# Attention weights copied by DMA to float32r tiles and transposed as float32r, in pairs 1 to 6

## The chip, the core and the metric

The kernel runs on one core of one Trainium2 chip. The metric is the device time of one execution in microseconds (us). Before the change it is 680.45 us, the median of three runs (680.29 to 680.69).

## The reference

One layer over a sequence of 1024 positions and a width of 1024. A normalised and modulated input goes through one combined projection into two groups of eight heads of width 64. Both groups compute causal attention in blocks of 128 queries; each block makes a matrix of weights, 128 queries by up to 1024 keys, and multiplies it with the values (forgetting attention first, then stick-breaking):

```python
s = jnp.einsum('bhqd,bhkd->bhqk', q, k).astype(jnp.float32) * scale
s = s + (f_q[..., :, None] - f_k[..., None, :])
causal = k_pos[None, :] <= q_pos[:, None]
s = jnp.where(causal, s, -jnp.inf)
p = jax.nn.softmax(s, axis=-1)
return jnp.einsum('bhqk,bhkd->bhqd', p.astype(v.dtype), v)
...
later = lax.cumsum(log_keep, axis=3, reverse=True) - log_keep
w = jnp.where(strict, jnp.exp(log_beta + later), 0.0)
return jnp.einsum('bhqk,bhkd->bhqd', w.astype(v.dtype), v)
```

The gated head outputs go through one output projection, are added to the residual with a gate, and are normalised.

## The kernel before

The sixteen heads are worked on as eight pairs. Pairs 0 to 3 are stick-breaking, pairs 4 to 7 forgetting attention. A unit is (pair, head in the pair, block of 128 queries); there are 128 units, 16 in a pair. Block i of a unit sees (i + 1) x 128 keys, so a unit's weights are a tile of 128 rows and 128 to 1024 columns.

TensorE's order is written out by hand: one loop over turns k (at the end of `tile_hybrid_layer`). In a turn of pairs 0 to 3 `weights_turn(k)` comes first, then `scores_turn(k)`, then a piece of the projections of later pairs ("fill"; tiles `m` at L312 to L314 and `v` at L370 to L372). In a turn of pairs 4 to 7 the scores come first, then a fill, then the weights, then another fill. `scores_turn(k)` issues the score products of unit k into PSUM tile S (L483, L484). `weights_turn(k)` transposes the weights of unit k - 2 (LAG = 2; L537, into PSUM tile T, four blocks of 128 x 128 to a tile) and multiplies with the values what is complete (L554).

Between scores and transposes a unit runs through the other engines:

- pairs 0 to 3: ScalarE makes two sigmoids (L506 to tile kp, L508 to tile be), VectorE scans kp (L514, L518), GpSimd multiplies be by kp (L520) and zeroes one column (L521, which may stand ahead of L520). Then be is what is transposed.
- pairs 4 to 7: VectorE adds the forget row fb and finds the row's extreme (L491, to tile a), ScalarE exponentiates (L496), VectorE takes a reciprocal (L497), GpSimd scales (L499). Then a is what is transposed.

A transpose is a TensorE product in transpose mode: the block of weights is loaded as the stationary operand (LDWEIGHTS, the rows PEld), a 128 x 128 identity in float32 is streamed through it. ScalarE then rounds T to float32r (L539, tile pt), and VectorE takes what is left over (L540).

The tiles kp, be, a, and the forget rows fb share one tag with six buffers ("att", 128 x 1024 float32 each). The order of the instructions on the other engines, and of the DMAs on the queue of SyncE (SP), is made by a scheduler when the kernel is built. That queue is first in, first out: a DMA that waits for its data holds up those behind it. It carries weight loads (`raw`, L123), copies of keys within SBUF (L298), finished outputs (`y_dr`, L578) and, in pairs 4 to 6, the output weights (`raw_o`, and `wo_dr` at L896, L897).

Of the kernel before, what the change touches and what calls it, by code (L numbers as in the profile page):

```python
# [7 lines left out]

F32 = mybir.dt.float32
F32R = mybir.dt.float32r  # L10
AF = mybir.ActivationFunctionType
ALU = mybir.AluOpType

P = 128
# [3 lines left out]
NPAIR = 8  # L18
# [5 lines left out]
BIG = 3.0e38  # L24
# [3 lines left out]
def tile_hybrid_layer(  # L28
# [17 lines left out]
    nc = tc.nc  # L46

    cp = ctx.enter_context(tc.tile_pool(name="const", bufs=1))
# [4 lines left out]
    def big(tag, bufs, name, dt=F32, shape=None):  # L53
        return sb.tile(shape or [P, 1024], dt, tag=tag, bufs=bufs, name=name)

    def att_tile(name, dt=F32):
        return big("att", 6, name, dt)

    def pt_tile(name, dt=F32R, shape=None):
        return big("pt", 3, name, dt, shape or [P, 2, 1024])  # L60
# [7 lines left out]
    def t_tile(name):  # L68
        return ps.tile([P, 512], F32, tag="T", bufs=2, name=name)

    def s_tile(name):
        return ps.tile([P, 2, 512], F32, tag="S", bufs=1, name=name)
# [11 lines left out]
    def after(*instructions):  # L84
        stack = ExitStack()
        for i in instructions:
            stack.enter_context(tc.issue_after(i.ins))
        return stack


    ident = cp.tile([P, P], F32, tag="ident", name="ident")
    make_identity(nc, ident)
    causal = cp.tile([P, P], F32, tag="causal", name="causal")
    nc.gpsimd.memset(causal, 0.0)
    nc.gpsimd.affine_select(out=causal, in_=causal, pattern=[[-1, P]], base=0,
                            channel_multiplier=1, compare_op=ALU.is_ge, fill=MASKED)
# [9 lines left out]
    gate = cp.tile([P, D], F32, tag="gate", name="gate")  # L106
# [339 lines left out]
    st_w, st_pt = {}, {}  # L446
# [4 lines left out]
    def att_query(u):  # L451
# [3 lines left out]
        r = slice(h * HD, h * HD + HD)  # L455
        nc.scalar.copy(z[r, :], qst[p][h].bitcast(F32)[r, i * P:i * P + P])  # L456

    masks, scaled, lows, gates = [], [], [], []

    def att_causal(u):  # L460
        p, h, i = u
        if p >= 4:
            if not masks:
                masks.append(pv_tile("causal_ps", 1)[:, :P])
                nc.vector.tensor_copy(masks[0], causal)
            f = fb[2 * (p - 4) + h]
            dg = slice(i * P, i * P + P)
            nc.vector.tensor_tensor(f[:, dg], f[:, dg], masks[0], op=ALU.add)

    def att_scores(u, following):  # L470
        p, h, i = u
        z = zq.pop(u)
        ke = (i + 1) * P
        ns = 1 if ke <= 512 else 2
        w = ke // ns
        qs = slice(i * P, i * P + P)
        if p >= 4:
            f = fb[2 * (p - 4) + h]
        S = s_tile(f"S_{p}_{h}_{i}")
        halves = range(ns) if p >= 4 else range(ns)[::-1]  # L480
        for s in halves:
            ks = slice(s * w, s * w + w)
            nc.tensor.matmul(S[:, s, :w], qst[p][h][:, qs], kst[p][h][:, ks], start=True, stop=False)  # L483
            nc.tensor.matmul(S[:, s, :w], z, klo[p][:, ks], start=False, stop=True)  # L484
        v3 = lambda a: a[:, :ke].rearrange("p (a b) -> p a b", a=ns)
        if p >= 4:
            a = att_tile(f"a_{p}_{h}_{i}")
            nm = sb.tile([P, 1], F32, tag="nm", bufs=4, name=f"nm_{p}_{h}_{i}")
            l = sb.tile([P, 1], F32, tag="l", bufs=4, name=f"l_{p}_{h}_{i}")
            with after(*lows):  # L490
                nc.vector.tensor_tensor_reduce(out=v3(a), in0=S[:, :ns, :w], in1=v3(f),  # L491
                                               op0=ALU.add, op1=ALU.min, scale=-1.0, scalar=BIG,
                                               accum_out=nm)
            if following:
                att_causal(following)
            nc.scalar.activation(a[:, :ke], a[:, :ke], AF.Exp, scale=-1.0, bias=nm, accum_out=l)  # L496
            nc.vector.reciprocal(l, l)  # L497
            scaled[:] = [*scaled[-3:],
                         nc.gpsimd.tensor_scalar(a[:, :ke], a[:, :ke], l, 1.0, op0=ALU.mult, op1=ALU.mult)]  # L499
            st_w[u] = a  # L500
        else:
            kp = att_tile(f"kp_{p}_{h}_{i}")
            be = att_tile(f"be_{p}_{h}_{i}")
            with after(*key_casts):
                for s in halves:
                    nc.scalar.activation(kp[:, s * w:s * w + w], S[:, s, :w], AF.Sigmoid, scale=-1.0)  # L506
            key_casts.clear()
            last_act = nc.scalar.activation(v3(be), S[:, :ns, :w], AF.Sigmoid)  # L508
            gates[:] = [last_act]


            lo = ke - w
            rv = kp[:, lo:ke][:, ::-1]
            last_dve = nc.vector.tensor_tensor_scan(rv, rv, floor[:, :ke - lo], initial=0.0,  # L514
                                                    op0=ALU.mult, op1=ALU.max)
            if lo:
                rv = kp[:, :lo][:, ::-1]
                last_dve = nc.vector.tensor_tensor_scan(rv, rv, floor[:, P:P + 1].to_broadcast([P, lo]),  # L518
                                                        initial=kp[:, lo:lo + 1], op0=ALU.mult, op1=ALU.max)
            nc.gpsimd.tensor_tensor(be[:, :ke - 1], be[:, :ke - 1], kp[:, 1:ke], op=ALU.mult)  # L520
            nc.gpsimd.memset(be[:, ke - 1:ke], 0.0)  # L521
            st_w[u] = be
            return last_act, last_dve

    def att_transpose(u, between=()):
        p, h, i = u
        a = st_w.pop(u)
        j, qo = i // 2, (i % 2) * P
        for g in range((i // 4) + 1):
            n = min(4, i + 1 - 4 * g)  # L530
            if (p, h, j, g) not in st_pt:
                st_pt[p, h, j, g] = pt_tile(f"pt_{p}_{h}_{j}_{g}", F32R, [P, 2, 4, 256])
            hi, lo = (st_pt[p, h, j, g][:, x] for x in range(2))
            tp = t_tile(f"T_{p}_{h}_{i}_{g}")
            for b in range(n):
                kb = 4 * g + b
                nc.tensor.transpose(tp[:, b * P:(b + 1) * P], a[:, kb * P:(kb + 1) * P], ident)  # L537
            t3 = tp[:, :n * P].rearrange("p (a b) -> p a b", a=n)
            nc.scalar.copy(hi[:, :n, qo:qo + P], t3)  # L539
            lows[:] = [nc.vector.tensor_tensor(lo[:, :n, qo:qo + P], t3, hi.bitcast(F32)[:, :n, qo:qo + P],  # L540
                                               op=ALU.subtract)]
            while between:
                att_pv(*between.pop(0))
# [3 lines left out]
    def att_pv(p, h, j):  # L547
        acc = pv_tile(f"pv_{p}_{h}_{j}")
        last = 2 * j + 1
        acc2 = acc.rearrange("p (a b) -> p a b", a=2)  # L550
        for kb in range(last + 1):
            pt = st_pt[p, h, j, kb // 4][:, :, kb % 4]
            q0 = P if kb == last else 0
            nc.tensor.matmul(acc2[:, :, q0:], vt[p][:, kb, h * P:(h + 1) * P], pt[:, :, q0:],  # L554
                             start=(kb == 0), stop=(kb == last))
        if p < 4:
            summed.append((acc, p, h, j))
        else:
            att_sum(acc, p, h, j)
# [276 lines left out]
    for kb in range(NB):  # L836
# [9 lines left out]
        if kb < len(evacs):  # L846
            n, h = evacs[kb]
# [237 lines left out]
    def weights_turn(k):  # L1085
        if LAG <= k < len(units) + LAG:
            u = units[k - LAG]
            att_transpose(u, ready)
            seen.add(u)
            if (u[0], u[1], u[2] ^ 1) in seen:  # L1090
                ready.append((u[0], u[1], u[2] // 2))
        while k >= len(units) + LAG and ready:
            att_pv(*ready.pop(0))
# [106 lines left out]
```

## Time and profile before

| what | value |
|---|---|
| median of three runs | 680.45 us |
| span of the profiled execution | 678.6 us |
| TensorE matmul busy | 668.3 us (98%) |
| TensorE weight loads busy | 571.2 us (84%) |
| VectorE, ScalarE, GpSimd busy | 485.9, 382.6, 405.2 us |
| transposes of attention weights | 576 |
| DMAs issued by SP | 294 |

The profiled execution's own time is not listed apart from its span: the span runs from its first to its last instruction, and the median of the three runs is 1.85 us above it, which is taken for what lies around it. Matmuls are pipelined and their ends are modelled, so the starts of successive matmuls tell what one costs, not their busy time. The merged rows of a timeline give the start, the time from the first start to the last end, and how many instructions a row holds.

### The profile page before, as it was taken

The numbers are of one execution on the slowest core, as the hardware profiler recorded it, in microseconds if no ns is written. First come the engines' busy times: TensorE is split into PE (matmuls) and PEld (weight loads), VectorE is DVE, ScalarE is ACT, GpSimd is POOL, SyncE is SP. The second block draws the span as 40 slices with busy tenths as digits, with TensorE's granted clock in tenths as the row PEclk, the third lists the DMA queues.
The fourth block names the chain that finished last, engine by engine and source line by source line (L and its number), as shares of the span: only waits on it lengthen the run. The fifth ranks groups of instructions, "written<-read, shape, count | busy, mean of one in ns | idle before, by whom it ended". The sixth has DMA issues, their size and how long they took to land.

```text
span 678.6 us, 11231 instructions
## 1 busy us (share of the span) xinstructions
PE 668.3 (98%) x3713; PEld 571.2 (84%) x3713; DVE 485.9 (72%) x1001; ACT 382.6 (56%) x889; POOL 405.2 (60%) x530
## 2 busy tenths in 40 slices
PE   8999999999999999999999999999999999999995
PEld 4888898888998888889988888889988888888885
DVE  6787779868677777686776675766676777775645
ACT  5576468757567667576675564655565766521000
POOL 5560279755357556556378878785785365655412
PEclk9999999999999999999999999999999999999998
DMA  9983432112101112122124555263452297153301
GB/s 326 401 312 126 139 79 75 41 28 67 29 20 56 54 42 57 40 54 56 49 93 144 151 164 174 87 201 112 127 169 59 70 350 302 59 177 107 120 32 63
DMA packets 46474, 81.55 MB, mean 120 GB/s; under 512 B 5264, under 2 KB 20176, under 8 KB 46416
## 3 DMA queue, kind: packets, MB, share of 16 engines
q1 hardware_dynamic: 44832, 76.37, 35.1%
q10 hardware_dynamic: 1584, 4.47, 2.1%
q8 instruction: 29, 0.48, 0.3%
q14 instruction: 29, 0.24, 0.1%
HBM read 60.34 MB, written 16.29 MB: 113 GB/s over the span
## 4 chain that ended last, share of the span: by engine, by line
PE 97%; DMA 1%; DVE 0%; POOL 0%; ACT 0%; issue 0%; SPq 0%; POOLq 0%
PE m L312 11%; PE m L314 10%; PE m L313 10%; PE pv L554 10%; PE T L537 9%; PE S L484 5%; PE S L483 5%; PE o L939 4%; PE o L937 4%; PE o L938 4%; PE v L370 4%; PE v L372 4%; PE v L371 4%; PE st_q L647 1%; PE st_k L647 1%; PE st_late L647 1%
## 5 line engine op out<-in xcount | busy, mean ns | idle before, releaser
L540 DVE TENSOR_TENSOR pt<-T,pt 128x512 fp32r<-128x512 f32 (+2 forms) x192 | 102.7, 553 | 43.8 <-ACT pt L539 42.2
L539 ACT CAST pt<-T 128x512 fp32r<-128x512 f32 (+2 forms) x192 | 88.9, 479 | 64.5 <-PE T L537 62.5
L312 PE MATMUL m<-uh,whi 128*128 128x512 f32 x304 | 123.3, 405 | 0.1
L314 PE MATMUL m<-uh,wlo 128*128 128x512 f32 x304 | 119.8, 394 | 0.0
L313 PE MATMUL m<-ul,whi 128*128 128x512 f32 x304 | 119.7, 394 | 0.0
L520 POOL TENSOR_TENSOR be<-be,kp 128x127 f32<-128x127 f32 (+3 forms) x64 | 78.9, 1234 | 36.2 <-DVE kp L518 24.4
L554 PE MATMUL pv<-pt,v 128*128 128x512 f32 x320 | 82.8, 388 | 0.0
L514 DVE TENSOR_TENSOR_SCAN kp<-kp,floor 128x128 f32<-128x128 f32 (+3 forms) x64 | 58.6, 915 | 17.6 <-ACT kp L506 17.4
L499 POOL TENSOR_SCALAR a<-a,l 128x1024 f32<-128x1024 f32 (+3 forms) x64 | 48.4, 756 | 34.3 <-DVE l L497 26.0
L483 PE MATMUL S<-k,q 128*128 128x512 f32 (+5 forms) x192 | 68.8, 360 | 0.0
L314 PEld LDWEIGHTS m<-uh,wlo 128*128 128x128 f32 x304 | 57.1, 188 | 13.7
L496 ACT ACTIVATE a<-a,nm 128x1024 f32<-128x1024 f32 (+3 forms) x64 | 49.8, 779 | 28.6 <-DVE nm L491 28.1
L312 PEld LDWEIGHTS m<-uh,whi 128*128 128x128 f32 x304 | 57.2, 188 | 10.2 <-PE T L537 0.3
L484 PE MATMUL S<-kl,qz 128*128 128x512 f32 (+5 forms) x192 | 65.2, 341 | 0.0
L313 PEld LDWEIGHTS m<-ul,whi 128*128 128x128 f32 x304 | 57.3, 188 | 9.0
L554 PEld LDWEIGHTS pv<-pt,v 128*128 128x128 f32 x320 | 55.5, 189 | 8.9
L570 POOL TENSOR_TENSOR ty<-ty,sg 64x256 f32<-64x256 f32 x64 | 46.9, 733 | 23.4 <-issue 12.2
L491 DVE CUSTOM_DVE_ANT_0 a<-S,fb 128x1024 f32<-128x1024 f32 (+3 forms) x64 | 48.2, 753 | 16.9 <-PE S L484 12.0
L456 ACT CAST qz<-q 64x128 fp32r<-64x128 f32 x128 | 37.3, 296 | 34.2 <-PE S L484 33.0
L506 ACT ACTIVATE kp<-S 128x384 f32<-128x384 f32 (+4 forms) x96 | 44.0, 494 | 21.5 <-PE S L484 20.2
L370 PE MATMUL v<-whi_v,uh 128*128 128x256 f32 (+1 forms) x192 | 54.7, 285 | 0.0
L372 PE MATMUL v<-wlo_v,uh 128*128 128x256 f32 (+1 forms) x192 | 54.2, 282 | 0.0
(296 smaller groups left out, 1628.3 us busy)
## 6 DMA issues: line engine op xcount, KB each, us to landing
raw<-in_w_qkg_dram SPq DMA_DIRECT2D x38, 256.0 KB, 2.7
wss<-in_w_ss_dram SPq DMA_DIRECT2D x14, 512.0 KB, 8.1
x<-in_x_dram SPq DMA_DIRECT2D x8, 512.0 KB, 7.1
k<-k SPq DMA_DIRECT2D x32, 128.0 KB, 2.3
wg<-in_w_gate_dram SPq DMA_DIRECT2D x8, 512.0 KB, 4.9
raw_o<-in_w_out_dram SPq DMA_DIRECT2D x16, 256.0 KB, 3.0
fb<-f_dr ACTq DMA_DIRECT2D x8, 512.0 KB, 4.5
wo_dr<-whi_o SPq DMA_DIRECT2D x16, 256.0 KB, 2.1
```

Source lines behind the costliest of these rows:

```text
L312: nc.tensor.matmul(acc, hi[:, c], u_hi[kt][:, s], start=(kt == 0), stop=False)
L313: nc.tensor.matmul(acc, hi[:, c], u_lo[kt][:, s], start=False, stop=False)
L314: nc.tensor.matmul(acc, lo[:, c], u_hi[kt][:, s], start=False, stop=(kt == NB - 1))
L370: nc.tensor.matmul(acc[:, :n], u_hi[kt][:, ts_], hi[:, s], start=(kt == 0), stop=False)
L372: nc.tensor.matmul(acc[:, :n], u_hi[kt][:, ts_], lo[:, s], start=False, stop=(kt == NB - 1))
L483: nc.tensor.matmul(S[:, s, :w], qst[p][h][:, qs], kst[p][h][:, ks], start=True, stop=False)
L484: nc.tensor.matmul(S[:, s, :w], z, klo[p][:, ks], start=False, stop=True)
L520: nc.gpsimd.tensor_tensor(be[:, :ke - 1], be[:, :ke - 1], kp[:, 1:ke], op=ALU.mult)
L537: nc.tensor.transpose(tp[:, b * P:(b + 1) * P], a[:, kb * P:(kb + 1) * P], ident)
L539: nc.scalar.copy(hi[:, :n, qo:qo + P], t3)
L540: lows[:] = [nc.vector.tensor_tensor(lo[:, :n, qo:qo + P], t3, hi.bitcast(F32)[:, :n, qo:qo + P], op=ALU.subtract)]
L554: nc.tensor.matmul(acc2[:, :, q0:], vt[p][:, kb, h * P:(h + 1) * P], pt[:, :, q0:], start=(kb == 0), stop=(kb == last))
```

## The change

- In pairs 1 to 6 (`HOPS`), each unit's finished weights are copied by a DMA of the SP queue from be or a to another tile of the same tag, declared float32r (`hop`). The copy moves the bytes of (i + 1) x 128 columns as they are.
- The transposes of these pairs read the copy and the identity as float32r and write T as float32r. Pairs 0 and 7 stay as they were.
- The identity is made by the same two GpSimd operations as in the helper used before, written through a float32r tile.
- One unit, (2, 0, 1), is transposed a second time in float32, and the difference of the two, times 3e38, is added to the gate: one more PSUM tile, two transposes, one ScalarE and two VectorE operations.

```diff
+    ident_r = cp.tile([P, P], F32R, tag="ident", name="ident")
+    ident = ident_r.bitcast(F32)
...
+    HOPS = range(1, NPAIR - 1)
+
+    def hop(u, w, ke):
+        if u[0] not in HOPS:
+            return w
+        to = att_tile(f"w_{u[0]}_{u[1]}_{u[2]}", F32R)
+        nc.sync.dma_start(to.bitcast(F32)[:, :ke], w[:, :ke])
+        return to
...
-            st_w[u] = a
+            st_w[u] = hop(u, a, ke)
...
-            st_w[u] = be
+            st_w[u] = hop(u, be, ke)
...
-                nc.tensor.transpose(tp[:, b * P:(b + 1) * P], a[:, kb * P:(kb + 1) * P], ident)
+                if p in HOPS:
+                    nc.tensor.transpose(tp.bitcast(F32R)[:, b * P:(b + 1) * P], a[:, kb * P:(kb + 1) * P], ident_r)
+                else:
+                    nc.tensor.transpose(tp[:, b * P:(b + 1) * P], a[:, kb * P:(kb + 1) * P], ident)
+            if u == (2, 0, 1):
+                tq = t_tile("T_again")
...
+                nc.scalar.copy(ta[:, w], tq[:, w])
+                nc.vector.tensor_tensor(ta[:, w], tp[:, w], ta[:, w], op=ALU.subtract)
+                nc.vector.scalar_tensor_tensor(gate[:, w], ta[:, w], BIG, gate[:, w], op0=ALU.mult, op1=ALU.add)
```

The six buffers now hold in pairs 1 to 3 two of kp, two of be and two copies w, and in pairs 4 to 6 two forget rows, two of a and two copies; each kind takes turns. So a of unit k takes the buffer of a of unit k - 2, which is free once that one's copy has landed.

The queue of SP around the end of pair 1, before: weight loads for pair 3 (`raw_3_...`, the load, its module and half), and outputs of pair 1 (`y_dr`).

```order
L123 DMA raw_3_1_0_2815<-in_w_qkg_dram 128x512
L578 DMA y_dr_91<-ty_1_1_1_2376 64x256
L123 DMA raw_3_1_1_2821<-in_w_qkg_dram 128x512
L123 DMA raw_3_2_0_3003<-in_w_qkg_dram 128x512
L578 DMA y_dr_91<-ty_1_1_2_2490 64x256
L123 DMA raw_3_2_1_3009<-in_w_qkg_dram 128x512
```

The same place in the changed kernel; `w_1_1_6` is the copy of unit (1, 1, 6).

```order
L125 DMA raw_3_1_0_2870<-in_w_qkg_dram 128x512
L466 DMA w_1_1_6_2404<-be_1_1_6_2396 128x896
L602 DMA y_dr_91<-ty_1_1_1_2406 64x256
L125 DMA raw_3_1_1_2876<-in_w_qkg_dram 128x512
L125 DMA raw_3_2_0_3066<-in_w_qkg_dram 128x512
L466 DMA w_1_1_7_2470<-be_1_1_7_2462 128x1024
L466 DMA w_2_0_0_2522<-be_2_0_0_2516 128x128
L602 DMA y_dr_91<-ty_1_1_2_2524 64x256
```

The copies stand between the loads; that of unit (1, 1, 7) stands behind two weight loads.

VectorE at the start of pair 6, before: the reduction of unit (6, 0, 5) (`a_6_0_5`), and the work on the transposes of units (5, 1, 0) and (6, 0, 7) (`pt_... <- T_...`).

```order
L540 TENSOR_TENSOR pt_5_1_0_0_5877<-T_5_1_0_0_5920,pt_5_1_0_0_5877 128x128
L491 ISA a_6_0_5_5946,nm_6_0_5_5947<-S_6_0_5_5941,fb_4_5291 128x768
L491 ISA nm_6_0_5_5947 128x1
L305 SCALAR_TENSOR_TENSOR sg_6_5869<-sg_6_5869,m_6_2_1_5870 128x512
L468 TENSOR_TENSOR fb_4_5291<-fb_4_5291,causal_ps_4030 128x128
L497 RECIPROCAL l_6_0_5_5948<-l_6_0_5_5948 128x1
L540 TENSOR_TENSOR pt_6_0_3_0_5959<-T_6_0_7_0_5960,pt_6_0_3_0_5959 128x4x128
```

The same place in the changed kernel:

```order
L564 TENSOR_TENSOR pt_5_1_0_0_6046<-T_5_1_0_0_6091,pt_5_1_0_0_6046 128x128
L479 TENSOR_TENSOR fb_4_5442<-fb_4_5442,causal_ps_4133 128x128
L508 RECIPROCAL l_6_0_6_6076<-l_6_0_6_6076 128x1
L307 SCALAR_TENSOR_TENSOR sg_6_6038<-sg_6_6038,m_6_2_1_6039 128x512
L564 TENSOR_TENSOR pt_6_0_3_0_6132<-T_6_0_7_0_6133,pt_6_0_3_0_6132 128x4x128
L502 ISA a_6_0_5_6117,nm_6_0_5_6118<-S_6_0_5_6112,fb_4_5442 128x768
L502 ISA nm_6_0_5_6118 128x1
```

The reduction of unit (6, 0, 5) moved behind the first half of the transposed unit (6, 0, 7), whose copy frees the buffer that it writes. The same holds of units (4, 1, 4), (6, 0, 4) and (6, 1, 4). TensorE's order is as before but for the two more transposes.

More of the change, by code (lines that the diff above doesn't have):

```diff
@@ L5 @@
 from concourse import mybir
-from concourse.masks import make_identity
 from concourse._compat import with_exitstack
@@ L88, in after @@
         return stack
-    ident = cp.tile([P, P], F32, tag="ident", name="ident")
-    make_identity(nc, ident)
+    ident_r = cp.tile([P, P], F32R, tag="ident", name="ident")
+    ident = ident_r.bitcast(F32)
+    nc.gpsimd.memset(ident, 0.0)
+    nc.gpsimd.affine_select(out=ident_r, in_=ident, compare_op=ALU.not_equal, fill=1.0, base=0,
+                            pattern=[[-1, P]], channel_multiplier=1)
     causal = cp.tile([P, P], F32, tag="causal", name="causal")
@@ L536, in att_transpose @@
                 kb = 4 * g + b
-                nc.tensor.transpose(tp[:, b * P:(b + 1) * P], a[:, kb * P:(kb + 1) * P], ident)
+                if p in HOPS:
[4 more added lines that the diff above has]
+                tq = t_tile("T_again")
+                for b in range(n):
+                    kb = 4 * g + b
+                    nc.tensor.transpose(tq[:, b * P:(b + 1) * P], a.bitcast(F32)[:, kb * P:(kb + 1) * P], ident)
+                ta = att_tile("T_both")
+                w = slice(0, n * P)
+                nc.scalar.copy(ta[:, w], tq[:, w])
+                nc.vector.tensor_tensor(ta[:, w], tp[:, w], ta[:, w], op=ALU.subtract)
+                nc.vector.scalar_tensor_tensor(gate[:, w], ta[:, w], BIG, gate[:, w], op0=ALU.mult, op1=ALU.add)
             t3 = tp[:, :n * P].rearrange("p (a b) -> p a b", a=n)
```

## The prediction

> **What bounds the kernel now.** First the profile's page: the share of each engine, the clock, and the chain that ended last.
>
> ```profile
> span 678.6 us, 11231 instructions
> PE 668.3 (98%) x3713; PEld 571.2 (84%) x3713; DVE 485.9 (72%) x1001; ACT 382.6 (56%) x889; POOL 405.2 (60%) x530
> PEclk9999999999999999999999999999999999999998
> PE 97%; DMA 1%; DVE 0%; POOL 0%; ACT 0%; issue 0%; SPq 0%; POOLq 0%
> PE m L312 11%; PE m L314 10%; PE m L313 10%; PE pv L554 10%; PE T L537 9%; PE S L484 5%; PE S L483 5%; PE o L939 4%; PE o L937 4%; PE o L938 4%; PE v L370 4%; PE v L372 4%; PE v L371 4%; PE st_q L647 1%; PE st_k L647 1%; PE st_late L647 1%
> ```
>
> The chain is TensorE for 97%, at full clock, and the attention transposes (T L537) are 9% of it. So whatever TensorE is spared counts in full, as long as nothing makes it wait, and every wait that is added counts in full too. Next the busy time by stage, for pairs 1 to 3 (136 to 342 us) and 4 to 6 (342 to 546 us), the two stretches that the change touches.
>
> ```profile
> 136.00:342.00 206.00, 206.00 (x1230) 181.71 (x1229) 152.08 (x261) 135.85 (x328) 118.05 (x164) 1.00 0.18 47
> 342.00:546.00 204.00, 203.95 (x1141) 175.56 (x1141) 139.74 (x366) 120.69 (x293) 149.46 (x170) 1.00 0.44 131
> ```
>
> The columns are the stretch, its length, then busy time of PE, PEld, DVE, ACT, POOL, the clock, the DMA engines' share and GB/s. TensorE has no gap in either; the other engines have a quarter or more of their time free. The view of waits says how near a gap is:
>
> ```profile
> PEld T L537 <- POOL be L520: 1.3, 4, 0.4
> ```
>
> All waiting of TensorE for finished weights is 1.3 us in the whole run. What matters is therefore how early the weights are finished, since the copy comes in between.
>
> **The transposes.** The chain of waits gives what each product costs from one start to the next, around the end of pair 1; then load and product durations by line (LDWEIGHTS is the load; xcount | busy, mean ns | idle), and the one float32 product of 128 columns that is no transpose (L185).
>
> ```profile
> 208.25 0.33 PE T L537 x3
> 208.58 0.06 PE S L483
> 208.64 0.11 PE S L484
> 208.75 0.28 PE m L312
> ...
> 211.35 0.24 PE m L314
> 211.59 0.87 PE T L537 x8
> ```
>
> ```profile
> L484 PEld LDWEIGHTS S<-kl,qz 128*128 128x128 f32 x192 | 36.3, 189 | 3.3
> L537 PEld LDWEIGHTS T<-ident,be 128*128 128x128 f32 x288 | 34.7, 141 | 7.1 <-POOL be L520 1.3 <-POOL be L521 0.4 <-issue 0.3
> ```
>
> ```profile
> L185 PE MATMUL sc_all<-ident,sc x16: 273/275/275, 6.5 to 8.2; 128*128 128x128 f32 x16
> ```
>
> Eight transposes take 0.87 us: 0.109 each. Pairs 1 to 6 have 6 x 2 x 36 = 432, so 47.1 us. A float32r product of 512 columns takes 0.24, so 128 columns stream in 0.06; the transpose streams the same 128 columns in float32 and takes nearly twice that. The other bound is S with 128 columns in float32r: the two S and the excess of the m behind them (0.28 against 0.23 to 0.24) are 0.06 + 0.11 + 0.05 = 0.22 for two, 0.11 each. There it isn't streaming but loads that follow each other, and a load of S takes 189 ns. A transpose's load takes 141, that is 48 less, so at 0.11 the load leaves room and the float32 stream is what fills the time. I take 0.06 (rounded up from 0.058), nearest to the row of 512 columns: **432 x (0.109 - 0.060) = 21.2 us saved**. The ends are 0.11 (nothing saved) and 0.06; a loss is excluded, since S shows float32r with a load of its own for each 128 columns at 0.11. The Trainium skill (FP8 and Floating Point Precision, TensorE Precision Notes) says that true float32 takes four passes through the array, which by quarters would make a transpose 0.027 and the saving 35.4 us; this trace speaks against it, for L185 shows two products for each of the 8 turns of its loop and T L537 one for each transpose (576). The second transpose of unit (2, 0, 1) adds two float32 transposes, 0.2 us, and small work on ScalarE and VectorE; I count 0.3 us. The identity is made by the same two operations: nothing.
>
> **The copies.** Each of 96 units gets a DMA between GpSimd's last step and the first transpose. No 128-row copy inside SBUF is in the trace; the nearest rows (KB each, median us from issue to landing):
>
> ```profile
> fb<-f_dr ACTq DMA_DIRECT2D x8, 512.0 KB, 4.5
> k<-k SPq DMA_DIRECT2D x32, 128.0 KB, 2.3
> out_dram<-r SPq DMA_DIRECT2D x2, 512.0 KB, 2.8
> y_dr<-ty SPq DMA_DIRECT2D x56, 64.0 KB, 1.9
> ```
>
> The same direction is k<-k, 2.3 for 128 KB. From 64 to 512 KB writes out of SBUF rise by 0.9. With 0.1 for the hand-over and the load ahead of the first product I take **c = 2.2 + 1.2 x columns/1024**: 2.35 us for 64 KB, 3.4 for 512 KB. The low end is 2.0 + 0.8 (out_dram), the high end 2.5 + 2.4 (fb, 4.5 for 512 KB, and 0.4 to start).
>
> Against this stands the slack: from the end of GpSimd's last operation on a unit to the start of its first transpose. Four units, GpSimd's rows and TensorE's rows:
>
> ```profile
> 203.08 1.77 POOL L520 TENSOR_TENSOR be<-be,kp 128x895 f32<-128x895 f32 x1 [0.55 <-DVE kp L518]
> 208.32 2.00 POOL L520 TENSOR_TENSOR be<-be,kp 128x1023 f32<-128x1023 f32 x1
> 367.00 0.69 POOL L499 TENSOR_SCALAR a<-a,l 128x512 f32<-128x512 f32 x1
> 492.47 1.14 POOL L499 TENSOR_SCALAR a<-a,l 128x1024 f32<-128x1024 f32 x1
> ```
>
> ```profile
> 206.36 0.60 PE L537 MATMUL T<-ident,be 128*128 128x128 f32 x4
> 211.42 1.03 PE L537 MATMUL T<-ident,be 128*128 128x128 f32 x8
> 374.23 0.60 PE L537 MATMUL T<-ident,a 128*128 128x128 f32 x4
> 495.09 0.60 PE L537 MATMUL T<-ident,a 128*128 128x128 f32 x4
> ```
>
> Unit (1, 1, 6) is ready at 204.85 and transposed from 206.36: slack 1.5, c 3.25. Unit (1, 1, 7): 210.32 and 211.42, 1.1 against 3.4. Unit (4, 0, 3): 367.69 and 374.23, 6.5 against 2.8; it is covered. Unit (6, 0, 7): 493.61 and 495.09, 1.5 against 3.4. I read the slack of all 96 units in this way. The short ones are blocks 6 and 7 in pairs 1 to 3 (0.4 to 1.9 us, the last head of pair 3 excepted), whose chain over four engines is longest, and the start of pair 6; blocks 0 to 4 mostly have 2.5 to 6, and pairs 4 and 5 mostly 4 to 8.
>
> A stall of TensorE moves all that follows on it, so a stall at the unit between a unit's scores and its transposes lengthens that unit's slack. Hence: stall = c + wait in the queue - slack - the stall at the units between + what faster transposes there (0.049 each) bring it forward. (1, 1, 6): unit (1, 1, 5) before it stalls 0.9, with 6 transposes: 3.25 - 1.5 - 0.9 + 0.3 = 1.1. (1, 1, 7) has a wait in the queue as well; its copy now stands behind two weight loads:
>
> ```profile
> 208.26 3.68 SPq L123 DMA_DIRECT2D raw<-in_w_qkg_dram  x2
> ```
>
> The second ends at 211.94 and an issue takes 0.33, so the copy can't start before 211.6, 1.3 after its data: 3.4 + 1.3 - 1.1 - 1.1 + 0.3 = 2.8. (6, 0, 7): 3.4 - 1.5 + 0.1 = 2.1. In pairs 4 to 6 there is one more wait: a of unit k needs the buffer whose copy is k - 2.
>
> ```profile
> 494.69 0.96 DVE L491 CUSTOM_DVE_ANT_0 a<-S,fb 128x768 f32<-128x768 f32 x1 [0.84 <-PE S L484]
> ```
>
> This is unit (6, 0, 5) at 494.69; the copy of (6, 0, 7) lands at 493.61 + 3.4 = 497.0, and by the new order the reduction stands behind the first half of that unit's transposed tile besides, to about 498.7. So this unit is 4 us later, and (6, 0, 5) and (6, 0, 3) together stall 6.3. Summed over the pairs 1 to 6: **8.1 + 9.0 + 2.7 + 2.2 + 1.5 + 9.5 = 33.0 us of stalls**. With low c it is 24.5, with high c 63; without a saving on the transposes, nothing brings them forward and it is 26.7. Without waits in the queue and for buffers it is 22.8.
>
> What is queued behind a waiting copy on SP: weight loads, key copies, outputs. By the starts in the trace and the new order some go up to 4 to 5 us later in pair 5, output weights above all. I cost this at nothing: such waits stand in the queue already, and the products that use the weights don't wait.
>
> ```profile
> SPq L123 <- POOL wlo L128: 49.7, 22, 6.1
> SPq L578 <- POOL ty L570: 158.3, 45, 10.3
> L312 PE MATMUL m<-uh,whi 128*128 128x512 f32 x304 | 123.3, 405 | 0.1
> ```
>
> If that cover goes, each late load is a stall of its length.
>
> **The sum.** Span 678.6, and 1.85 around it make the median of 680.45. -21.2 (transposes) + 0.3 (the unit done twice) + 33.0 (stalls) = +12.1: **692.5 us**.
>
> **Rivals.**
> A is the forecast: transposes at 0.06, stalls that outweigh it. Its own range by c is 684 (24.5 of stalls) to 714 (c nearer its high end).
> B: the transposes stay at 0.11. For: the S pair at 0.11, and an element of four bytes in and out as before. Against: the load of 141. Then 680.45 + 0.3 + 26.7 = 707.4. The Trainium skill (TensorE: Matmul & The Clock Gate, LDWEIGHTS) gives a load as its columns over 1.2 GHz, which for 128 is 107 ns whatever the product streams; by that rule this rival is what happens. The rows of S agree with it, the shorter load of T doesn't.
> C, the other sign: faster. The copies run at the low end (2.0 + 0.8) and the scheduler's order costs nothing, as the queue and buffer waits that I count come from starts that shift along; then stalls are 15.5 and the time 680.45 - 21.2 + 0.3 + 15.5 = 675.1. It decides for faster where stalls stay below 20.9. For: pairs 4 and 5 have slack to spare. Against: blocks 6 and 7 of pairs 1 to 3 lack 1.5 to 3 us each at any price of a DMA in the trace, the smallest of which is 1.9.
> D: transposes at a quarter. Then saved 35.4, stalls 38.2 as slack shrinks further: 680.45 - 35.4 + 0.3 + 38.2 = 683.6.
>
> **How the numbers follow.** A 0.47, B 0.32, C 0.12, D 0.05, and 0.04 for a sum that comes out between A and C, within 0.2% (1.4 us, about what a measurement of this kernel can tell from no change). Slower is A + B + D = 0.84, faster C = 0.12, same 0.04. The range runs from 682, below A and D, to 716, which takes in B and most of slow copies; it leaves out C, and some 0.07 of B with copies near 4.5 us.
>
> **What would show it.** In the profile after, T L537 from start to start: 0.06 (A), 0.11 (B), 0.03 (D). PEld T L537 waiting for the DMA of w: 30 us or so in some 25 waits, most before blocks 5 to 7 of pairs 1 and 2 and early in pair 6, few in pairs 4 and 5; under 20 would mean C. The copies to landing: 2.2 to 3.3 us. VectorE's L502 in pair 6 waiting for a copy or for pt. The forecast is wrong if TensorE waits mostly for something else (weights of m, the values), or if the stalls sit in pairs 4 and 5, or if a float32r transpose costs more than 0.11.

## The result, and the profile after

The changed kernel takes **726.84 us** (median of 4 runs, 725.86 to 732.51) against 680.37 before (median of 4 runs as well): ratio 1.0699, 95% interval 1.0663 to 1.0736. It is slower, as forecast, but by 46.5 us where 12.1 were forecast, and above the upper end of the range (716). The profiled execution has a span of 725.1, 46.5 more than before; the rest is read from it.

The page of the changed kernel: the busy times, the clock, and the chain that ended last.

```profile
span 725.1 us, 11557 instructions
PE 677.0 (93%) x3715; PEld 570.1 (79%) x3715; DVE 488.2 (67%) x1003; ACT 383.5 (53%) x890; POOL 405.3 (56%) x530
PEclk9999999999999899999999999999999999999998
PE 68%; DMA 12%; issue 7%; POOL 7%; DVE 3%; ACT 3%; SPq 0%; POOLq 0%; DVEq 0%; ACTq 0%
```

VectorE, ScalarE and GpSimd have the busy times of before. TensorE is at 93% instead of 98%, and the chain runs through other engines for a third of its length. The same two stretches of time as before the change (columns as there):

```profile
136.00:342.00 206.00, 187.55 (x1069) 159.92 (x1068) 138.87 (x234) 122.24 (x292) 109.53 (x151) 0.98 0.30 99
342.00:546.00 204.00, 189.63 (x1110) 162.92 (x1108) 126.73 (x318) 110.17 (x268) 142.40 (x160) 0.98 0.56 188
```

TensorE, which had no gap in either, is idle for 18 and 14 us, and the clock is 0.98 instead of 1.00. Who is waited for stands in the groups by line and shape (xcount | busy, mean ns | idle time before and its releasers):

```profile
L549 PE MATMUL T<-ident,w 128*128 128x128 f32 x432 | 52.9, 241 | 26.0 <-DMA w<-be 15.8 <-DMA w<-a 9.2 <-DVE kp L529 0.8
L494 PE MATMUL S<-k,q 128*128 128x512 f32 x48 | 21.2, 441 | 2.9 <-DVE nm L502 2.7 <-ACT be L519 0.2
L372 PE MATMUL v<-whi_v,uh 128*128 128x256 f32 x128 | 37.3, 291 | 2.4 <-POOL whi_v L129 2.4
```

The view counts a product as busy to its modelled end, 0.16 us after the next one could have started. From start to start a wait costs that much more, so the 26.0 us before the transposes are about 30. Summed in this way over all products of the two traces, the 46.5 us are (where a product both waits and runs at half clock the line between two terms can be drawn otherwise, which shifts them by up to 0.3):

| term | us | forecast |
|---|---|---|
| waits before T (22 of them, 29.7 us, for a copy in pairs 1 to 6) | +29.9 | +33.0 |
| other waits: S 4.4, fcum 4.2, v 3.6, pv 1.6, the rest 0.6 | +14.4 | 0 |
| products that run at half clock | +8.3 | 0 |
| the transposes themselves, with the unit done twice | -6.4 | -20.9 |
| end of the kernel | +0.3 | 0 |

Each of the 22 waits for a copy ends when that copy has landed: the first transpose starts 0.04 to 0.14 us after the landing in the trace.

### The profile page after: what moved, and what is told of

It reads as the page before. It is cut to its first block, busy times and chain, and to the rows that moved or that the text cites. A ratio compares the mean times of both kernels' runs of the same rounds, so it can differ in the third digit from the quotient of the medians.

```text
span 725.1 us, 11557 instructions
## 1 busy us (share of the span) xinstructions
PE 677.0 (93%) x3715; PEld 570.1 (79%) x3715; DVE 488.2 (67%) x1003; ACT 383.5 (53%) x890; POOL 405.3 (56%) x530
## 4 chain that ended last, share of the span: by engine, by line
PE 68%; DMA 12%; issue 7%; POOL 7%; DVE 3%; ACT 3%; SPq 0%; POOLq 0%; DVEq 0%; ACTq 0%
PE pv L578 8%; PE m L314 6%; PE m L316 6%; PE m L315 6%; PE o L963 4%; PE o L961 4%; PE o L962 4%; DMA w<-be 4%; PE S L494 4%; PE S L495 3%; PE T L549 3%; DMA wss<-in_w_ss_dram 3%; DMA w<-a 3%; PE v L372 3%; PE v L374 3%
## 5 line engine op out<-in xcount | busy, mean ns | idle before, releaser
L549 PEld LDWEIGHTS T<-ident,w 128*128 128x128 f32 x432 | 47.5, 142 | 42.0 <-issue 14.2
L549 PE MATMUL T<-ident,w 128*128 128x128 f32 x432 | 52.9, 241 | 26.0 <-DMA w<-be 15.8
L502 DVE CUSTOM_DVE_ANT_0 a<-S,fb 128x1024 f32<-128x1024 f32 (+3 forms) x64 | 48.3, 755 | 17.8 <-PE S L495 10.2
L532 POOL MEMSET be<- 128x1 f32 x64 | 6.3, 99 | 95.3 <-ACT be L519 85.1
```

The lines of the kernel that those rows point to most:

```text
L549: nc.tensor.transpose(tp.bitcast(F32R)[:, b * P:(b + 1) * P], a[:, kb * P:(kb + 1) * P], ident_r)
```

## The experiments

All times are medians of 4 or more runs beside runs of the kernel before (680.4). Theory P in the expectations is the table above, with 8.0 us for the type of the transposes where nothing waits; A and B are the prediction's own.

### What the type is worth, without copies

```
+    def wt(u, w):
+        to_w[u] = att_tile(f"w_{u[0]}_{u[1]}_{u[2]}", F32R) if u[0] in HOPS else w
+        return to_w[u]
...
-        nc.sync.dma_start(to.bitcast(F32)[:, :ke], w[:, :ke])
...
-            nc.gpsimd.tensor_tensor(be[:, :ke - 1], be[:, :ke - 1], kp[:, 1:ke], op=ALU.mult)
+            to = wt(u, be)
+            nc.gpsimd.tensor_tensor(to[:, :ke - 1], be[:, :ke - 1], kp[:, 1:ke], op=ALU.mult)
```

The second kernel has the same edit with w in F32 and every transpose with `ident`.

> GpSimd's last operation writes its result straight into the float32r tile w (its values are rounded to float32r, which the change itself does not do), so there is no copy; transposes stay float32r, buffers and the double unit stay. Theory P (from the trace after: a group of n transposes costs 22 ns less for each transpose beyond the first, 8.0 us in all, and all the rest of the loss comes from the copies): no wait of TensorE for w, 672 to 675 us. The record's A (49 ns saved on each of 432): 659 to 662. The record's B (nothing saved): 680 to 683. If the loss comes from the buffer that w takes and not from the copy, this kernel is slower than 690.

> As the kernel in which GpSimd writes w itself, but w is plain float32 and every transpose is float32: no copy, no float32r. It differs from that one in the type alone. P: 680 to 683, 8 us above it. A: 21 us above it. B: the same as it.

Measured: **682.81** (ratio 1.0040, 1.0025 to 1.0055) and **687.72** (1.0107, 1.0087 to 1.0127). P's time misses for both, by 8 and by 5 us: it had all the rest of the loss come from the copies, and the waits of other products that are left without a copy make 7.2 and 5.0 us, counted as in the table. The first time lies where B would have it, but not for B's reason. What P said of the wait holds: TensorE waits 0.0 us for w in both, so all of that wait comes with the copies, and without them 2.4 us of the 46.5 are left. The type is worth 4.9 us in the time (A had 21, B nothing); the products alone, counted as in the table, differ by about 7. Unit (2, 0, 7), first in float32r, then in float32, from the timelines of the two:

```profile
249.98 0.80 PE L554 MATMUL T<-ident,w 128*128 128x128 f32 x8
250.61 0.35 PE L498 MATMUL S<-k,q 128*128 128x256 f32 x1
```

```profile
252.07 1.03 PE L556 MATMUL T<-ident,w 128*128 128x128 f32 x8
252.86 0.36 PE L498 MATMUL S<-k,q 128*128 128x256 f32 x1
```

From the first transpose to S it is 0.63 against 0.79. In float32r the first three start 0.06 and 0.07 apart, near the forecast, and the next ones 0.083 to 0.089: there each product starts about 0.036 after its own load, and the loads start 0.083 to 0.088 apart. In float32 each load starts with the product before it, 0.108 apart. So in float32r the load is what the products follow, at 0.085 and not at 0.06. What the 0.108 of float32 is made of these rows don't settle: that it was the stream, as the prediction argued, isn't shown, since the S behind the last float32 transpose starts only 0.03 after it. A group saves about 23 ns for each transpose beyond its first; the 432 transposes stand in 120 groups without another product between, so that is 312 x 0.023 = 7.2 us, which fits the 7. The Trainium skill (TensorE: Matmul & The Clock Gate, Back-to-back issue gap) gives about 81 ns for each product in a stream of loads and products of 128 columns; the trace is near it with 83 to 89 for these transposes, not with the 0.11 of the prediction's S.

Not expected: the second kernel has no copy and no float32r and is still 7.3 us slower than before (2.9 of it at half clock). Beside the double unit it only takes one more attention buffer for each unit of these pairs. That is an effect of its own, below.

### The copies alone

```
-        to = att_tile(f"w_{u[0]}_{u[1]}_{u[2]}", F32R)
+        to = att_tile(f"w_{u[0]}_{u[1]}_{u[2]}")
...
-                if p in HOPS:
+                if False:
```

> The copies alone: w is a plain float32 tile, filled by the same 96 transfers, and all transposes are float32 as before. P: the changed kernel's 726.8 plus the 8 us that the type saves, less or more a few us for stalls that shift, 730 to 740. A: 748 (21 us above). B: 727, the same.

Measured: **725.74**, and wide (719.61 to 729.57; why its runs differ by 10 us was not settled). P's 730 to 740 misses; it is what B would give. Its profiled run, the slowest of the four, is 2.8 us longer than that of the changed kernel: the products cost 7.7 more and half clock 1.9 more, but the waits for w are 26.9 us from start to start instead of 29.7, and other waits are about 4 less. Where TensorE waits for the weights anyway, a shorter transpose only lengthens the next wait, so in the presence of the copies little of what the type saves reaches the end; how little, four runs that differ by 10 us don't tell.

### The copy's price

```
         nc.sync.dma_start(to.bitcast(F32)[:, :ke], w[:, :ke])
+        nc.sync.dma_start(to.bitcast(F32)[:, :ke], w[:, :ke])
```

> The changed kernel with each copy made twice into the same tile, the second waiting for the first; the transposes wait for both. P (the price is the latency between GpSimd's last operation and the transposes): each copy lands about 2.5 us later, one stall for about every two units where the slack is used up, waits of T for w from 30 to 70 to 95 us, more stretches at half clock, 765 to 800. Rival (the stalls come from the order of instructions and the buffers, which stay as they are): waits of T up by less than 10 us, 727 to 740.

Measured: **805.33** (ratio 1.1832), 5 us above P's range and far from the rival's. The transposes' group:

```profile
L550 PE MATMUL T<-ident,w 128*128 128x128 f32 x432 | 57.3, 255 | 85.9 <-DMA w<-be 42.7 <-DMA w<-a 41.6 <-DVE kl L301 1.3
```

From 26.0 to 85.9 us, about 93 from start to start, in 45 waits. The same units with twice the latency wait three times as long. This run alone doesn't single out the latency: SP stands longer at each pair of copies, and the scheduler's order on VectorE, ScalarE and GpSimd is not the same. But the first copy of a pair is still issued 0.03 us after its data in the median, and the waits end with the landings. So the price is the time from GpSimd's last operation to the first transpose.

```
-        nc.sync.dma_start(to.bitcast(F32)[:, :ke], w[:, :ke])
+        nc.gpsimd.dma_start(to.bitcast(F32)[:, :ke], w[:, :ke])
```

> The changed kernel with the 96 copies issued on GpSimd's queue, right behind the operation that writes their data; SP's queue is as before the change. P (the price of a copy is its latency; the place on SP's queue is the smaller part): waits of T for w fall from 30 to 22 to 25 us, waits for weights of the values (3.6) go, 712 to 720. Rival Q (the queue is the greater part): waits of T under 15 us, below 705. Rival R (a transfer issued on GpSimd lands later or keeps GpSimd busy): above 727.

Measured: **751.37** (1.1050), far above P's 712 to 720, and R holds: GpSimd's row went from 405.3 to 458.8, 0.56 us for each of the 96 issues. The copies are issued 0.8 us after their data in the median, where SP issues them 0.03 after, and TensorE's idle time before the transposes is 42.8 us instead of 26.0. So this run doesn't tell what the place in SP's queue is worth.

```profile
PE 686.8 (92%) x3715; PEld 576.5 (77%) x3715; DVE 488.6 (65%) x1003; ACT 382.2 (51%) x890; POOL 458.8 (61%) x626
```

But SP's queue was hardly late in the first place. In the changed kernel 92 of the 96 copies are issued within 0.6 us of their data, most 0.03 after it; SP stands at the copy and waits for GpSimd (and what is behind it, weight loads among it, waits too). Of the 22 stalls only that of unit (4, 1, 6), 1.2 us, has a copy that stood long in the queue (2.0 us). SP's waits there, us, times, longest:

```profile
SPq L466 <- POOL be L531: 72.6, 41, 3.7
SPq L466 <- ACT be L519: 40.0, 25, 3.7
SPq L466 <- POOL a L510: 34.6, 31, 3.1
```

### The forget gate's scratch tile

TensorE's longest single wait in the changed kernel is not for a copy. GpSimd's timeline there, and TensorE's:

```profile
237.43 1.54 POOL L531 TENSOR_TENSOR be<-be,kp 128x767 f32<-128x767 f32 x1 [1.17 <-DVE kp L529]
238.94 0.62 POOL L129 TENSOR_SCALAR whi<-raw 128x512 fp32r<-128x512 f32 x1
239.49 0.20 POOL L425 MEMSET fscratch<- 128x128 f32 x1
239.66 1.26 POOL L130 TENSOR_TENSOR wlo<-raw,whi 128x512 fp32r<-128x512 f32 x1
240.88 0.29 POOL L426 TENSOR_SCALAR_AFFINE_SELECT fscratch<-fscratch 128x128 f32<-128x128 f32 x1
```

```profile
241.22 0.69 PE L429 MATMUL fcum<-flf,fscratch 128*128 128x64 f32 x2 [4.08 <-POOL fscratch L426]
```

The scratch tile is an attention buffer. With w in the same six buffers it comes free later, and the new order has its memset behind be of block 5 (the first row above). Before the change it stood ahead of it:

```profile
228.26 0.20 POOL L423 MEMSET fscratch<- 128x128 f32 x1
231.46 1.55 POOL L520 TENSOR_TENSOR be<-be,kp 128x767 f32<-128x767 f32 x1 [1.15 <-DVE kp L518]
```

TensorE, whose order still has fcum at the old place, waits 4.1 us.

```
-        scratch = att_tile("fscratch")
+        scratch = sb.tile([P, 512], F32, tag="ty", bufs=2, name="fscratch")
```

> The changed kernel, but the scratch tile of the forget gate comes from the two buffers of the output tile ty in place of the attention buffers. P: its memset goes back ahead of block 4's be on GpSimd, the 4.1 us wait of the product fcum goes and with it the half-clock stretch of 6.8 us behind it (about 2.8 us of loss): 726.8 - 4.2 - 2.8 = about 720. Rival: the transposes behind it wait in its place, since their copies are late anyway: 725 to 727, with a wait of T of about 3 us at 241 us.

Measured: **720.49** (1.0589, 1.0573 to 1.0606), 6.3 us less, as P said. The memset is at 229.10, before block 5's be and block 4's as well, fcum follows without a wait, and the half-clock stretch behind it is gone:

```profile
229.10 0.20 POOL L425 MEMSET fscratch<- 128x128 f32 x1
229.38 0.29 POOL L426 TENSOR_SCALAR_AFFINE_SELECT fscratch<-fscratch 128x128 f32<-128x128 f32 x1
```

The same edit on the kernel without copies:

> GpSimd writes w itself in float32r, as in the kernel without copies, and the scratch tile comes from the ty buffers. P: its wait of fcum (3.1 us) and the half clock behind it (1.4) go: 682.8 - 4.5 = 678, faster than before by 0.3%. Rival: another wait takes its place, 681 to 683.

Measured: **678.15** (0.9968, 0.9956 to 0.9979): faster than before, by as much as P said.

### Where the slack was long

```
-    HOPS = range(1, NPAIR - 1)
+    HOPS = (4, 5)
```

> The change in pairs 4 and 5 alone (the double unit is then two float32 transposes). P: a third of the saving on the transposes (2.1 to 2.7 us), waits of T for w of 3 us or so as these pairs have them in the changed kernel, and waits for S and for the weights of the values of 3 to 5: 681 to 686. Rival: without the late pairs 1 to 3 ahead of it the slack of 4 to 8 us covers all copies, and the kernel is faster than before, 677 to 679.

Measured: **687.73** (1.0109), above P's upper end, and the rival falls. The forecast's slack was right in the main: all waits for w of the two pairs make 1.5 us. But S waits 2.0, v 2.7, pv about 1.5, and half clock takes 1.6. The longest wait for S, with VectorE's rows and then TensorE's:

```profile
398.33 0.69 DVE L564 TENSOR_TENSOR pt<-T,pt 128x512 fp32r<-128x512 f32 x1 [2.08 <-ACT pt L563]
398.94 0.81 DVE L502 CUSTOM_DVE_ANT_0 a<-S,fb 128x640 f32<-128x640 f32 x1
```

```profile
397.21 0.73 PE L549 MATMUL T<-ident,w 128*128 128x128 f32 x7
399.91 0.47 PE L494 MATMUL S<-k,q 128*128 128x512 f32 x1 [1.21 <-DVE nm L502]
```

The copy of unit (4, 1, 6) lands at 396.75, in time for its transposes at 397.21. The reduction of unit (4, 1, 4) (L502) writes the buffer that this copy has freed, and in the new order it stands behind the first half of that transposed tile: VectorE is idle for 2.1 us before it, and the next S, which needs the tile that the reduction empties, waits 1.2. So the slack covers the latency of a copy; it doesn't cover the order that the buffer brings. How much of the S, v and pv waits is this was not tried apart.

### What is left without copy and without buffer

```
-            be = att_tile(f"be_{p}_{h}_{i}")
+            be = att_tile(f"be_{p}_{h}_{i}", F32R if p in HOPS else F32)
...
+            bf = be.bitcast(F32) if p in HOPS else be
+            nc.gpsimd.tensor_tensor(be[:, :ke - 1], bf[:, :ke - 1], kp[:, 1:ke], op=ALU.mult)
```

The lines above are those of the first of three kernels. In none of them is there a copy; the second takes in pair 0 and leaves out the double unit, and the third is the second with GpSimd writing a tile w of its own in pairs 4 to 6, which again takes a buffer.

> Pairs 1 to 3 alone, float32r without any further buffer: be itself is a float32r tile, ScalarE and GpSimd write it rounded, no copy. The double unit stays. It shows what the transposes are worth where nothing else moves. P: half of 7 to 8 us, less 0.4 for the double unit: 676.5 to 677.5. A: 670.2. B: 680.8.

> In pairs 0 to 3 be itself is float32r, written rounded, no copy; the double unit is left out. P: the 2.35 us of pairs 1 to 3, 0.4 for the double unit, and a little under a third of 2.7 for pair 0: 676.5 to 677.2. Rival: pair 0's transposes stand between products where nothing is saved: 677.6.

> As in place in pairs 0 to 3, and in pairs 4 to 6 GpSimd writes a float32r tile w of its own (rounded); no copy, no double unit. P: the saving of pairs 0 to 3 (3.5) and half of 7 us for pairs 4 to 6, less waits for S and for the weights of the values of 3 us that the further buffer brings: 675.5 to 677.5. Rival: these waits outweigh the saving: 678 to 680.

Measured: **678.03** (0.9965, 0.9952 to 0.9978), **676.29** (0.9943, 0.9927 to 0.9960) and **675.19** (0.9925, 0.9910 to 0.9939). The first is 0.5 above P's upper end (it has a wait of pv of 0.9 left); A's 670 is far off. The second and third come out just under P's lower end. The last one is 0.75% faster than the kernel before. Its page has TensorE back at 98%; what it pays is that the attention weights are rounded to float32r before the transpose, which the copy was there to avoid. No run here shows what that rounding does to the output.

```profile
span 673.5 us, 11222 instructions
PE 661.3 (98%) x3713; PEld 562.5 (84%) x3713; DVE 485.1 (72%) x1001; ACT 381.7 (57%) x889; POOL 405.6 (60%) x530
```

## Why the prediction was wrong

The sign was right, and the term that it worked out most came near: the stalls on the copies are 29.9 us where 33.0 were forecast, by pair 6.0, 6.8, 6.3, 1.2, 2.2 and 7.2 against 8.1, 9.0, 2.7, 2.2, 1.5 and 9.5. The copies of pairs 1 to 3 mostly land a little sooner than c, which was 2.35 for 64 KB and 3.4 for 512 with the hand-over in it; the smallest ones of pairs 4 to 6 land later (KB each, median us to landing):

```profile
w<-be SPq DMA_DIRECT2D x6, 512.0 KB, 3.0
...
w<-be SPq DMA_DIRECT2D x6, 64.0 KB, 1.8
w<-a SPq DMA_DIRECT2D x6, 64.0 KB, 4.3
```

That 22 waits end with a landing, and that twice the copy has three times the wait, shows that c less the slack is what is paid. That the sum of the stalls came so near is in part luck, as the last paragraphs of this section show. The miss of 34.3 us lies in three other steps.

- **"I take 0.06": 14.5 us.** A saving of 20.9 net was forecast; the products are 6.4 shorter. The step took the time of the stream for the time of the transpose. It compared a transpose's load (141 ns) with that of S (189 at 0.11) and concluded that the load leaves room. The loads of the transposes do follow each other faster than those of S, at 0.085, but that is still above 0.06. The right bound stood between the two ends that the text had, and the value taken was the end itself; in proportion to the two loads, 0.11 x 141 / 189 = 0.082 would have been an estimate from the same rows. Rival B, nothing saved, is 6.4 us off the other way, so nearer for the products, though with the copies in place the time hardly shows the difference.
- **"I cost this at nothing": 14.4 us.** The sum has stalls of the transposes alone. These words were said of what is queued behind a waiting copy, the only place where the text looks for other waits; the waits for S, fcum, v and pv make 14.4. No run shows a queued transfer to be their cause: in the two kernels with the extra buffer and no copy at all they are already 7.2 and 5.0. The one of 4.2 came from a place the prediction didn't look at, an unrelated tile that takes its turn in the same six buffers; the order of GpSimd's instructions showed it. The wait for S that was looked at comes from the reduction that moved behind a transposed tile, a step that the prediction has, but as stalls of the transposes in pair 6. The last load behind the waits for v was issued at 481.28, 0.03 after GpSimd had ended the operation ahead of it (`wlo_v`), and not behind a waiting copy. How the rest divides stays open.
- **The clock: 8.3 us.** The sum has no term for it. Three stretches of the profile, the middle one behind the wait for fcum (columns as above, the clock third from the end):

```profile
233.10:239.90 6.80, 4.04 (x21) 3.13 (x19) 3.94 (x5) 3.40 (x7) 3.81 (x7) 1.00 0.16 58
239.90:246.70 6.80, 5.48 (x19) 4.92 (x20) 0.98 (x2) 1.46 (x4) 1.27 (x2) 0.50 0.29 96
246.70:253.50 6.80, 6.18 (x31) 4.66 (x30) 6.29 (x9) 6.18 (x14) 4.19 (x5) 1.00 0.20 77
```

A wait of 4.1 us at 237 is followed by 6.8 us at half clock, the first 1.3 of them still waiting; 19 products run in it, 31 in the next stretch. The changed kernel has 20.5 us of this before its end.

Against these stand 3.1 us of stalls that didn't come, and 0.3 at the end: 14.5 + 14.4 + 8.3 - 3.1 + 0.3 = 34.4.

Inside the stalls several steps were wrong and hardly moved the sum. Unit (1, 1, 6) stalled 1.1 as forecast. But the wait in SP's queue for unit (1, 1, 7) (1.3 us) wasn't there, and it stalled 1.8 where 2.8 were forecast. Early in pair 6, where buffers and order should have made (6, 0, 5) and (6, 0, 3) stall 6.3 together, the first stalled 0.4 and the second not at all; (6, 0, 7) stalled 0.5 (the text's own terms, 3.4 - 1.5 + 0.1, make 2.0 and not 2.1). Instead two copies took far longer than c. The chain of waits shows unit (3, 1, 6), here with two loads on ScalarE's queue and the share of the DMA engines at that time (second column from the end):

```profile
361.34 7.30 DMA w<-be
```

```profile
360.90 0.34 ACTq L445 DMA_DIRECT2D fb<-f_dr  x1
361.27 0.45 ACTq L445 DMA_DIRECT2D fb<-f_dr  x1
```

```profile
364.00:367.00 3.00, 1.71 (x7) 1.06 (x7) 1.93 (x5) 0.56 (x2) 3.00 (x4) 1.00 0.92 287
367.00:370.00 3.00, 1.22 (x7) 1.10 (x8) 1.29 (x3) 0.58 (x1) 0.93 (x1) 0.93 1.05 404
```

The engines are full, and 448 KB take 7.3 us; the 64 KB of unit (6, 1, 0) took 7.7 in such a stretch. What stands beside both, and isn't in the prediction, is the load of forget rows fb, 512 KB each, on ScalarE's queue: two are issued just before the first of these copies and one 0.15 us behind the second. It shows in the other small copies as well: of the six of 64 KB in pairs 4 to 6, the five that were issued within 0.6 us of such a load landed 0.2 to 0.4 us after it and took 3.9 to 7.7 us; the sixth was issued 1.0 ahead of it and took 1.8. No run moved these loads, so that they are the cause is read from the times alone.

The two long copies cost 7.4 us together. Without them the stalls would be 22.5, which is the 22.8 that the text has without waits in the queue and for buffers. So the 29.9 is near 33.0 because a term that nobody had counted stands in for one that didn't come. Rival C needed stalls under 20.9, and D transposes at a quarter; neither is near.

## What to carry to other kernels

A transfer between two engines that already hand over just in time costs, at each unit, what its latency has over the slack, and then again what it brings with it: the buffer that it occupies, the instructions that the scheduler puts behind that buffer, and a clock that falls when TensorE runs dry. Its latency is that of the moment: look for large transfers that are issued beside it, on other queues too. When a product is made cheaper, ask what bounds it next (here the load of its weights) and look for a row between the two ends before taking the better one. If a type has to change, let the operation that makes the data write the new type: in pairs 1 to 6, with the scratch tile apart, that gave 0.3% where the copy lost 7%, and 0.75% with pair 0 and be in place, at the price of rounding.

## What the runs showed of the hardware

The half clock follows a rule that is simpler than the length of a wait. All stretches at half clock (but the one at each kernel's end) begin on a grid of 3.41 us and last 3.4 or 6.8. I cut the eight traces that have such stretches into windows of this grid and took TensorE's busy share of each, with the modelled ends of the view. Of more than 1500 windows at full clock, those at the kernels' starts and ends left out, 45 are followed by half clock: 43 of these are busy for less than half of the window, the other two for 52% and 56%. Of those that are followed by full clock only 2 are below half. So it needs no single long wait. The first row below is nearly the window of 52%, in the changed kernel: two waits for v of 2.4 and 0.8 us were enough, and TensorE is busy for 1.73 of 3.40 us:

```profile
485.60:489.00 3.40, 1.73 (x10) 1.48 (x11) 0.53 (x2) 0.27 (x1) 3.17 (x4) 1.00 0.26 71
489.00:492.40 3.40, 3.40 (x17) 3.36 (x16) 1.80 (x6) 1.93 (x5) 3.40 (x4) 0.51 0.65 243
```

The Trainium skill (TensorE: Matmul & The Clock Gate, Why this matters for your kernels) advises no idle gaps above about 3 us between bursts, and its section on the clock gate gives a free-running window of 3413 ns. The window agrees with these traces; the limit on gaps is too mild for them, since what goes with the half clock is about half a window idle, also in two pieces. No run set the busy share by itself, so the rule is one that the windows fit, with these four exceptions.
